# Layer 1's Hyena filter made in layer 1's mixing stage and kept on chip, both filters' inner layers made together

## The chip, the cores and the metric

The kernel runs on one core of a Trainium2 chip. The metric is the time of one execution on the device, in microseconds. The core's engines work side by side from queues in order: TensorE (PE, matrix products; its weight loads are PEld), VectorE (DVE), ScalarE (ACT), GpSimd (POOL) and SyncE (SP, which issues DMA loads). ACT also issues DMA stores.

## The reference

A trunk of two layers runs on two requests of 512 tokens, 1024 channels, with the same weights. Of each layer:

```python
h = _rmsnorm(x, norm_mix); proj = h @ w_in
q, k, v, g, hy_in, pool_in = jnp.split(proj, ...)
ret = _head_layernorm(_retention(q, k, v, logit_f, logit_b), ret_gn) * silu(g)
hy_out = _hyena(hy_in, ...)
pool_out = _pool_mixer(pool_in, pool_w, pool_scale)
x = x + concat([ret, hy_out, pool_out]) @ w_out
x = x + (gelu(dwconv3(h2 @ up_gate)) * (h2 @ up)) @ w_down      # h2 = _rmsnorm(x, norm_ffn)
x = x + sigmoid(x @ ple_gate_w) * _rmsnorm(p @ ple_w, ple_norm)
```

The Hyena group convolves 256 channels twice, by FFT, with filters that do not depend on the tokens. They come from a small network of each layer, and `khat` is their spectrum:

```python
h = sin(fr * (feats @ w1 + b1)); h = sin(fr * (h @ w2 + b2)); h = (h @ w3).reshape(L, 2, 2, 256)
h = h * exp(-t * deltas)
k_full = concat([h_f, 0, h_b[:0:-1]]); khat = rfft(k_full / sum(|k_full|))
```

Retention multiplies the scores of a head by decays `exp(dist * lg)`, which depend on the layer and head alone.

## The kernel before, in words

Every fp32 operand of a product is split into a high and a low f16 half, and a product is three matmuls (high by high, high by low, low by high; `mm3`, `pass3`). Weights of 128 x 1024 come by SP into `wraw` (4 buffers); ACT writes the high half and DVE the low one into `wspl` (9 buffers; `split`, lines 168 and 171). Tiles of 512 columns fp32 and halves of activations live in 72 buffers of the pool `gen`.

Each request has a `main_thread`, and side work has threads of its own: `filter_thread` and `decay_thread` of each layer, a `head_thread` per retention head, `hyena_thread`, `pool_thread`. All are generators. A planner (`schedule`) with a clock of its own takes the next step of the thread that is ready by planned times, and so writes the order of PE and of SP by hand; the order of DVE, ACT and POOL is set by the framework from the same program. A layer's tiles come in the order of `tile_order`: values `v00` to `v11` (PE: `vp`), then for heads 0 to 3 `q`, `k`, `g`, with the Hyena tiles `hy0` to `hy5` and the pooling tiles `pl0`, `pl1` between, the output tiles `o0` to `o7`, the gated FFN of both requests at once (`ffn_joint`), and the gate tiles `s0` to `s7` of the per-layer embedding.

A head: scores `sc`, times decays `st`, split `pt`, times values `ov`; then a layer norm over its 128 channels: ACT squares (`sq`), PE sums the columns (`cs`, line 753), DVE makes `rr`, PE spreads it (`rb`, line 763). The layer's own norm goes the same way, with `acc`, the sum of eight squares. Values are centred: `mu` and `vc` on DVE, high half of `v` on ACT, low half on DVE. The Hyena group transposes (`tp`), multiplies by Fourier matrices (`sp`), by `khat` on DVE, and back (`iv`).

`filter_thread(l)` loads feats, `fw` (w1, w2, b1, freq, b2) and w3, splits w3 (`w3s`), makes the first inner product (fp32, `fp`), then `sine` (six DVE operations and the sine on ACT), the second one and its sine, and splits the result (`h2`). Eight products with `w3s` follow; each is multiplied by `fdec` (`hfb`), its magnitudes are added (`fabs`, `ftot`), and sums and differences kept (`fs`, `fd`). A product with ones and a reciprocal give `frec`; the folds are multiplied by it and split (`folds`), and nine products with `fmat` give `khat`, written by ACT. Layer 0 makes its filter during its own mixing. Layer 1's is spawned by request 0's main thread of layer 0 at the tile named by `EARLY` (pl1); its nine `khat` of 256 KB are stored to DRAM (`ksp`) by ACT's queue, and `load_dft` loads them again by SP ahead of layer 1's first Hyena tile.

`decay_thread(l)` makes the tables of a layer, eight half heads: two DVE operations and an exponential on ACT for `dect`, and a store to DRAM (`ddec`) on ACT's queue. Layer 1's starts at planner time 425 (`run`: 25 + 400 l) and lies at about 465 to 517 us of the trace.

Of the kernel before, what the change touches and what calls it, by code (L numbers as in the profile page):

```python
# [16 lines left out]
F32 = mybir.dt.float32  # L17
# [14 lines left out]
JOINT = 3  # L32
HYW = 256
# [15 lines left out]
EARLY = "pl1"  # L49
# [47 lines left out]
def tile_order():  # L97

    names = ["v00", "v01", "v10", "v11"]
    for h, more in enumerate((["hy0", "hy1", "hy2", "hy3"], ["hy4", "hy5", "pl0"], ["pl1"], [])):  # L100
        names += [f"q{h}", f"k{h}", f"g{h}"] + more
    names += [f"o{m}" for m in range(NB)]
    for j in range(PLAIN):
        names += [f"fg{j}", f"fu{j}"]
    tiles, steps = list(names), list(names)
    pairs = []
# [15 lines left out]
    return tiles + more, steps + more  # L122
# [15 lines left out]
TILES, STEPS = tile_order()  # L138
TILE_AT = {n: i for i, n in enumerate(TILES)}
STEP_AT = {n: i for i, n in enumerate(STEPS)}  # L140
NT, NS = len(TILES), len(STEPS)


class Trunk:
# [54 lines left out]
    def plan_weights(self):  # L199
# [3 lines left out]
        for i in range(self.depth * NS):  # L203
            l, name = divmod(i, NS)
            name = STEPS[name]
# [24 lines left out]
    def prep(self, i):  # L230
# [5 lines left out]
        while k + 1 < len(self.at):  # L236

            frm = min(self.pos) if "." in STEPS[(k + 1) % NS] else i
# [16 lines left out]
    def wtile(self, l, last):  # L255
        self.live.append(l * NS + STEP_AT[last])
# [8 lines left out]
    def raw_names(self, j):  # L265

        return ("fg" + j[1:], "fu" + j[1:]) if j[0] == "f" else ("ea" + j[1:], "eb" + j[1:])
# [40 lines left out]
    def weight(self, l, name, *ss):  # L308
        i = l * NS + STEP_AT[name]
# [60 lines left out]
    def consts(self):  # L370
# [18 lines left out]
        self.ksp = self.dr.tile([9, 128, T], F32, name="ksp")  # L389
# [42 lines left out]
    def sine(self, a):  # L432

        k = self.g(name="sk")[0:64, :]
# [13 lines left out]
    def filter_thread(self, l, ev):  # L448
        nc, io = self.nc, self.io
        ft = self.g(name="feats")  # L450
        self.load(ft[0:33, :], io["feats"])
        fw = self.g(name="fw")
        self.load(fw[0:64, 0:132], io["fw"][l])
        w3 = []
        for o in range(2):
            w = self.g(name="w3")
            self.load(w[0:64, :], io["w3"][l][:, o * T:(o + 1) * T])
            q = self.g([128, 2, T], F16, name="w3s")
            self.split(q[0:64, 0], q[0:64, 1], w[0:64, :], WS)
# [4 lines left out]
        w1, w2, b1, fr, b2 = fw[0:33, 0:64], fw[0:64, 64:128], fw[0:64, 128:129], fw[0:64, 129:130], fw[0:64, 130:131]  # L464
        yield 0.0, 0.0
        a = self.g(name="fa")
        p = self.bank(name="fp")
        nc.tensor.matmul(p[0:64, :], w1, ft[0:33, :], start=True, stop=True)
        self.ts(a[0:64, :], p[0:64, :], b1, fr, ALU.add, ALU.mult)
        self.sine(a[0:64, :])  # L470
        yield 0.9, LAT["sin"][l > 0]
        a2 = self.g(name="fa2")
        p = self.bank(name="fp")
        nc.tensor.matmul(p[0:64, :], w2, a[0:64, :], start=True, stop=True)
        self.ts(a2[0:64, :], p[0:64, :], b2, fr, ALU.add, ALU.mult)
        self.sine(a2[0:64, :])
        a = None
        h2 = self.g([128, 2, T], F16, name="h2")
        self.split(h2[0:64, 0], h2[0:64, 1], a2[0:64, :])
        yield 0.9, LAT["sin"][l > 0]  # L480
# [62 lines left out]
        for i, (kind, pr, src) in enumerate(use):  # L543
# [19 lines left out]
        if l == 0:  # L563
            self.take_filters(kh)
# [89 lines left out]
    def load_dft(self, l):  # L654
        if l > 0:
            kh = {}
            for i, key in enumerate(FILTERS):
                kh[key] = self.g(name="khat")
                self.load(kh[key], self.ksp[i])
            self.take_filters(kh)  # L660
# [200 lines left out]
    def main_thread(self, s):  # L861
# [12 lines left out]
        for l in range(self.depth):  # L874
            vec = self.vec[l]
            h = []
            yield from self.h_steps(s, x, acc, vec[:, V_NMIX:V_NMIX + NB], h)
            x = None
            if s == 0 and l > 0:
                yield [self.ffn[l - 1].over]  # L880
            hw = self.hcw[l]
            mix = [None] * NB
            done = []
            hy, hev = [], [Event() for _ in range(6)]
            v = []
            for name in TILES[:TILE_AT["o0"]]:
                if name[0] == "v":
                    if name[2] == "0":
                        v.append([])
                        ps = self.values_early(l, h, s) if name == "v00" else [None, None]  # L890
                        for tp in range(2):
                            self.values(l, int(name[1]), h, s, tp, v[-1], ps.pop(0))
                            if ps or name != "v00":
                                yield (10.4 if name == "v00" else 5.2), 0.0
                    continue
                if name == "q0" and s == 0 and l > 0:
# [3 lines left out]
                p = self._proj(l, name, h, s)  # L900
                if name[:2] == "hy":
                    if name == "hy0" and s == 0:
                        self.load_dft(l)
                    j = int(name[2])
                    hy.append(self.conv3(p, hw, j, 6))
                    yield 5.15, 0.0
                    hev[j].set(self.clock + 3.0)
                    if j == 0:
                        done.append(Event())
                        self.spawn(self.hyena_thread(l, hy, hev, mix, done[-1]))  # L910
                elif name[:2] == "pl":
                    b = int(name[2])
                    if b == 0:
                        pw = self.g(name="poolw")
                        self.load(pw[:, 0:256], io["poolw"][l])
                    rc = self.g(name="rc")
                    self.load(rc, io["rcnt"][b])
                    m = self.pooling(p, b, rc)
                    yield 5.15, 0.0
                    done.append(Event())  # L920
                    self.spawn(self.pool_thread(l, b, m, None, pw[:, b * 128:(b + 1) * 128], mix, done[-1]))
                elif name[0] == "q":
                    qk = {"q": self.rotate(p)}
                    yield 5.15, 0.0
                elif name[0] == "k":
                    qk["k"] = self.rotate(p)
                    yield 5.15, 0.0
                else:
                    hd = int(name[1])
                    sg = self.g(name="sg")  # L930
                    self.act(sg, p, ACTF.Sigmoid, scale=1.0 / WS)
                    self.stt(sg, p, 1.0 / WS, sg, ALU.mult, ALU.mult)
                    if hd == 0:
                        yield [self.decay_ev[l]]
                    dec = self.dp.tile([128, 896], F32, tag="dec", name="dec")
# [542 lines left out]
```

## Time and profile before

| | us |
|---|---|
| runs | 2451.26, 2456.72, 2456.94 (median 2456.72) |
| profiled execution: its time | 2451.95 |
| its span | 2450.2 |
| PE busy | 2379.1 (97%) |
| DVE / ACT / POOL busy | 1779.5 / 1032.3 / 700.8 |
| mean DMA rate | 69 GB/s, 168.60 MB |

The span is what the profiler saw, from first to last instruction; the profiled execution took 1.75 us more. Engines overlap, so their busy times do not add up to the span. Mixing of layer 0 takes about the first 500 us, layer 1 begins at about 1246 us (its norm's column sum), its mixing ends near 1650. The granted clock of PE is given as a share of full speed.

### The profile page before, as it was taken

What the parts mean: (1) busy time and instruction counts of PE and PEld (TensorE: products, weight loads), DVE (VectorE), ACT (ScalarE), POOL (GpSimd) and SP (SyncE); (2) the same over time, 40 slices, a digit from 0 to 9 for tenths busy, and PEclk for the clock granted to TensorE, in tenths of its full rate; (3) what the DMA queues carried; (4) which work ended last, traced back from release to release, by engine and by line L of the source; (5) the groups of instructions that cost most, each with busy time, mean ns of one, the idle gap of its engine ahead of it and who ended that gap; (6) DMA issues with size and microseconds to landing.
All of it is one profiled execution on the core that took longest, in us unless ns stands there. A gap on an engine that the chain in (4) does not pass through costs nothing.

```text
span 2450.2 us, 30877 instructions
## 1 busy us (share of the span) xinstructions
PE 2379.1 (97%) x12024; PEld 1169.9 (48%) x12024; DVE 1779.5 (73%) x2526; ACT 1032.3 (42%) x1551; POOL 700.8 (29%) x528
## 2 busy tenths in 40 slices
PE   5999989999999999999999999999999999999997
PEld 4544654444444444444456555544444444444443
DVE  7994886968877868866575686554987786886655
ACT  4543334445534435444433343333553543544441
POOL 1213244124233333320121222510423334332011
PEclk8999999999999999999999999999999999999998
DMA  6122020341121121113232111032012112121301
GB/s 226 65 98 63 24 75 21 115 139 38 45 65 59 46 71 53 62 48 112 78 120 108 50 49 53 28 115 65 27 48 65 58 46 69 54 63 48 112 1 69
DMA packets 64363, 168.60 MB, mean 69 GB/s; under 512 B 7574, under 2 KB 13718, under 8 KB 64216
## 3 DMA queue, kind: packets, MB, share of 16 engines
q1 hardware_dynamic: 58312, 156.40, 19.3%
q10 hardware_dynamic: 5904, 10.23, 1.1%
q8 instruction: 94, 1.54, 0.3%
q14 instruction: 53, 0.43, 0.1%
HBM read 152.18 MB, written 14.42 MB: 68 GB/s over the span
## 4 chain that ended last, share of the span: by engine, by line
PE 74%; DVE 13%; issue 3%; ACT 2%; POOL 2%; DMA 0%; POOLq 0%; DVEq 0%; SPq 0%; ACTq 0%
PE fx L1183 13%; PE ex L1183 7%; PE fy L1183 7%; PE ey L1183 4%; PE fz L1183 3%; PE s L322 2%; PE o L323 2%; PE o L324 2%; PE o L322 2%; PE s L323 2%; PE s L324 2%; PE ez L1183 2%; DVE t L174 2%; DVE wspl L171 2%; DVE conv L171 2%
## 5 line engine op out<-in xcount | busy, mean ns | idle before, releaser
L1183 PEld LDWEIGHTS <-wspl 128*128 128x128 f16 x4704 | 461.1, 98 | 566.2 <-issue 13.7
L174 POOL TENSOR_TENSOR wraw<-wraw 128x512 f32<-128x512 f32 (+1 forms) x240 | 344.4, 1435 | 654.8 <-DVE wspl L171 640.7
L168 ACT ACTIVATE wspl<-wraw 128x1024 f16<-128x1024 f32 (+2 forms) x360 | 327.1, 910 | 370.8 <-POOL wraw L174 71.1
L171 DVE SCALAR_TENSOR_TENSOR wspl<-wraw,wspl 128x1024 f16<-128x1024 f32 (+2 forms) x360 | 395.5, 1100 | 82.6 <-ACT wspl L168 81.3
L1183 PE MATMUL fx<-hs,wspl 128*128 128x512 f16 x1368 | 312.3, 382 | 7.7 <-ACT r L168 7.7
L322 PEld LDWEIGHTS <-wspl 128*128 128x128 f16 x1536 | 152.1, 99 | 181.2 <-issue 6.9
L324 PEld LDWEIGHTS <-wspl 128*128 128x128 f16 x1536 | 150.6, 98 | 183.3 <-issue 3.3
L323 PEld LDWEIGHTS <-wspl 128*128 128x128 f16 x1536 | 150.7, 98 | 177.3 <-issue 3.6
L1183 PE MATMUL ex<-at,wspl 128*128 128x512 f16 x846 | 192.7, 379 | 0.0
L174 POOL TENSOR_TENSOR y<-t,mhalf 128x4 f32<-128x4 f32 x30 | 36.3, 1210 | 402.6 <-DVE t L178 402.5
L168 ACT ACTIVATE at<-conv 128x512 f16<-128x512 f32 x142 | 89.4, 629 | 143.7 <-DVE conv L174 111.8
L174 DVE TENSOR_TENSOR at<-conv,at 128x512 f16<-128x512 f32 x142 | 127.1, 896 | 26.2 <-ACT at L168 24.8
L171 DVE SCALAR_TENSOR_TENSOR conv<-r,scaled,conv 128x511 f32<-128x511 f32 x152 | 129.5, 852 | 2.1 <-ACT conv L168 0.4
L1183 PE MATMUL fx<-h,wspl 128*128 128x512 f16 x456 | 104.6, 379 | 0.0
L1183 PE MATMUL fy<-hs,wspl 128*128 128x512 f16 x456 | 104.6, 379 | 0.0
L1183 PE MATMUL fz<-h,wspl 128*128 128x512 f16 x456 | 104.6, 379 | 0.0
L1183 PE MATMUL fy<-h,wspl 128*128 128x512 f16 x456 | 104.6, 379 | 0.0
L168 ACT ACTIVATE sq<-x 128x512 f32<-128x512 f32 x80 | 49.2, 625 | 123.4 <-DVE x L171 66.3
L1183 PE MATMUL ey<-at,wspl 128*128 128x512 f16 x432 | 101.1, 379 | 0.0
L168 ACT ACTIVATE conv<-conv 128x512 f32<-128x512 f32 x88 | 55.3, 629 | 108.2 <-DVE conv L171 107.1
L174 DVE TENSOR_TENSOR acc<-acc,sq 128x512 f32<-128x512 f32 x84 | 62.6, 747 | 48.5 <-ACT sq L168 47.3
L324 PE MATMUL s<-xs,wspl 128*128 128x512 f16 x256 | 97.0, 379 | 0.0
(246 smaller groups left out, 4662.8 us busy)
## 6 DMA issues: line engine op xcount, KB each, us to landing
wraw<-in_w SPq DMA_DIRECT2D x172, 512.0 KB, 3.8
wraw<-in_w SPq DMA_DIRECT2D x48, 384.0 KB, 3.0
x<-in_x SPq DMA_DIRECT2D x32, 256.0 KB, 4.3
dec<-ddec SPq DMA_DIRECT2D x16, 448.0 KB, 4.6
wraw<-in_w SPq DMA_DIRECT2D x16, 256.0 KB, 2.6
xsp<-x ACTq DMA_DIRECT2D x16, 256.0 KB, 2.0
x<-xsp SPq DMA_DIRECT2D x16, 256.0 KB, 5.0
out_y<-out SPq DMA_DIRECT2D x16, 256.0 KB, 2.8
```

The lines of the kernel that those rows point to most:

```text
L168: return self.nc.scalar.activation(out=out, in_=in_, func=func, **k)
L171: return self.nc.vector.scalar_tensor_tensor(out=out, in0=in0, scalar=scalar, in1=in1, op0=op0, op1=op1)
L174: return (eng or self.nc.vector).tensor_tensor(out=out, in0=in0, in1=in1, op=op)
L322: self.nc.tensor.matmul(out, wv[:, 0, kb, :], x[:, 0], start=first, stop=False)
L323: self.nc.tensor.matmul(out, wv[:, 0, kb, :], x[:, 1], start=False, stop=False)
L324: self.nc.tensor.matmul(out, wv[:, 1, kb, :], x[:, 0], start=False, stop=last)
L1183: mm = lambda a, b, start=False, stop=False: self.nc.tensor.matmul(out, a, b, start=start, stop=stop, skip_group_check=not first)
```

## The change

The inner layers (w1, sine, w2, sine, split) of both filters are made at once in layer 0's filter thread: w1 of both layers side by side on 128 rows, w2 as blocks on the diagonal, one `fw` load of 128 x 259. `h2` of both layers is kept. Layer 1's filter thread starts with w3 and the first product with `w3s`; it is spawned in layer 1's own mixing, in request 0 at tile v10, and its `khat` stay on chip. In layer 1 the Hyena tiles come later: hy0 to hy3 after head 1, hy4, hy5, pl0 and pl1 after head 2. Layer 1's decay thread starts at planner time 1150. The code also gains a joint mixing of both requests (`mix_joint`, `TWINS`), which is off, since `TWINNED` is empty; `take` holds the steps of one tile that stood in `main_thread`.

```diff
-EARLY = "pl1"
+TWINNED = ()
+EARLY = "v10"
+LATER = 1125.0
...
-def tile_order():
+def tile_order(layer, twinned):
...
-    for h, more in enumerate((["hy0", "hy1", "hy2", "hy3"], ["hy4", "hy5", "pl0"], ["pl1"], [])):
+    late = ([], ["hy0", "hy1", "hy2", "hy3"], ["hy4", "hy5", "pl0", "pl1"], [])
+    for h, more in enumerate(late if layer else (["hy0", "hy1", "hy2", "hy3"], ["hy4", "hy5", "pl0"], ["pl1"], [])):
...
     def filter_thread(self, l, ev):
-        ft = self.g(name="feats")
-        self.load(ft[0:33, :], io["feats"])
-        fw = self.g(name="fw")
-        self.load(fw[0:64, 0:132], io["fw"][l])
+        rows = slice(l * 64, (l + 1) * 64)
+        if l == 0:
+            ft = self.g(name="feats")
+            self.load(ft[0:33, :], io["feats"])
+            fw = self.g(name="fw")
+            self.load(fw[:, 0:259], io["fw"])
         w3 = []
         for o in range(2):
             w = self.g(name="w3")
-            self.load(w[0:64, :], io["w3"][l][:, o * T:(o + 1) * T])
+            self.load(w[rows, :], io["w3"][l][:, o * T:(o + 1) * T])
             q = self.g([128, 2, T], F16, name="w3s")
-            self.split(q[0:64, 0], q[0:64, 1], w[0:64, :], WS)
+            self.split(q[rows, 0], q[rows, 1], w[rows, :], WS)
...
+        if l == 0:
+            w1, w2, b1, fr, b2 = fw[0:33, 0:128], fw[:, 128:256], fw[:, 256:257], fw[:, 257:258], fw[:, 258:259]
+            a = self.g(name="fa")
+            p = self.bank(name="fp")
+            nc.tensor.matmul(p, w1, ft[0:33, :], start=True, stop=True)
...
+            self.h2 = self.g([128, 2, T], F16, name="h2")
+            self.split(self.h2[:, 0], self.h2[:, 1], a2)
+            yield 0.9, LAT["sin"][0]
+        h2 = self.h2
...
-                self.pass3(p, h2[0:64, 0, jj], h2[0:64, 1, jj], w3[o][0:64, 0], w3[o][0:64, 1], True, True)
+                self.pass3(p, h2[rows, 0, jj], h2[rows, 1, jj], w3[o][rows, 0], w3[o][rows, 1], True, True)
...
-            if l > 0:
-                self.store(out=self.ksp[i], in_=kt)
-            else:
-                kh[kind, pr] = kt
+            kh[kind, pr] = kt
...
     def load_dft(self, l):
-        if l > 0:
-            kh = {}
-            for i, key in enumerate(FILTERS):
-                kh[key] = self.g(name="khat")
-                self.load(kh[key], self.ksp[i])
-            self.take_filters(kh)
...
+            for name in MIXING[l]:
+                if name == EARLY and s == 0 and l > 0:
+                    self.spawn(self.filter_thread(l, self.khat_ev[l]))
...
-                if name == EARLY and s == 0 and l + 1 < self.depth:
-                    self.spawn(self.filter_thread(l + 1, self.khat_ev[l + 1]))
...
-            self.spawn(self.decay_thread(l, self.decay_ev[l])).ready = 25.0 + 400.0 * l
+            self.spawn(self.decay_thread(l, self.decay_ev[l])).ready = 25.0 + LATER * l
```

How the order of the engines moves at two places follows. The first is ACT at the end of layer 0, where the squares of request 1's last two tiles feed the sum of the first norm of layer 1 (`sg` is the sigmoid of a gate tile, `s6` and `s7`; `xsp` a store). Before:

```order
L168 ACTIVATE sq_10522<-x_4856 128x512
L168 ACTIVATE sg_10552<-s6_10527 128x512
L168 ACTIVATE sq_10556<-x_4950 128x512
L184 DMA xsp_201<-x_4950 128x512
L168 ACTIVATE sg_10586<-s7_10561 128x512
L168 ACTIVATE sq_10590<-x_4995 128x512
L184 DMA xsp_201<-x_4995 128x512
L168 ACTIVATE v_10708<-vc_10706 128x512
```

In the changed program, from the square before (`sq_10185`) on:

```order
L181 ACT_TABLE_LOAD
L181 ACTIVATE dect_10173<-dect_10173 128x448
L181 ACT_TABLE_LOAD
L181 ACTIVATE sg_10215<-s6_10190 128x512
L197 DMA ddec_199<-dect_10173 128x448
L181 ACT_TABLE_LOAD
L181 ACTIVATE dect_10178<-dect_10178 128x448
L197 DMA ddec_199<-dect_10178 128x448
L181 ACTIVATE sq_10219<-x_4590 128x512
L197 DMA xsp_200<-x_4590 128x512
L181 ACT_TABLE_LOAD
L181 ACTIVATE sg_10249<-s7_10224 128x512
```

The exponentials of layer 1's decay tables, `dect`, stand between the squares and sigmoids, with four loads of ACT's tables of functions ahead of the last sigmoid.

The second place is DVE at the last values of layer 1 (`vp_10741` is one half of v10 of request 0), before:

```order
L738 TENSOR_REDUCE mu_10790<-vp_10741 128x4
L178 TENSOR_SCALAR mu_10790<-mu_10790 128x4
L171 SCALAR_TENSOR_TENSOR vc_10793<-vp_10741,mu_10790 128x512
L174 TENSOR_TENSOR v_10795<-vc_10793,v_10795 128x512
L738 TENSOR_REDUCE mu_10847<-vp_10798 128x4
L178 TENSOR_SCALAR mu_10847<-mu_10847 128x4
L171 SCALAR_TENSOR_TENSOR vc_10850<-vp_10798,mu_10847 128x512
L171 SCALAR_TENSOR_TENSOR hn_10864<-x_4426,vec1_94,rb_10855 128x512
L174 TENSOR_TENSOR v_10852<-vc_10850,v_10852 128x512
```

and in the changed program, where `vp_10414` is that tile:

```order
L745 TENSOR_REDUCE mu_10463<-vp_10414 128x4
L187 TENSOR_TENSOR v_10401<-vc_10399,v_10401 128x512
L191 TENSOR_SCALAR mu_10463<-mu_10463 128x4
L184 SCALAR_TENSOR_TENSOR vc_10466<-vp_10414,mu_10463 128x512
L187 TENSOR_TENSOR v_10468<-vc_10466,v_10468 128x512
L184 SCALAR_TENSOR_TENSOR w3s_10473<-w3_10471,w3s_10473 64x512
L184 SCALAR_TENSOR_TENSOR w3s_10478<-w3_10476,w3s_10478 64x512
L187 TENSOR_TENSOR hfb_10500<-fp_10496,fdec_10492 128x512
```

The low halves of w3 and the first `hfb` now stand behind the centred values, and the values of the next tile after them. PE in the changed program has at this place, with the end of `vp_10414` first:

```order
L341 LDWEIGHTS h_10170
L341 MATMUL vp_10414<-wspl_10273,h_10170 128x256
L342 LDWEIGHTS h_10170
L342 MATMUL vp_10414<-wspl_10273,h_10170 128x256
L340 LDWEIGHTS h2_529
L340 MATMUL fp_10496<-w3s_10473,h2_529 128x512
L341 LDWEIGHTS h2_529
L341 MATMUL fp_10496<-w3s_10473,h2_529 128x512
```

The first product of the filter follows directly on the tile `vp_10414`; before, the next `vp` did.

## Rows read from the trace of the kernel before

**Rows 1.** The page, first part: busy us (share of the span) of each engine.
```profile
PE 2379.1 (97%) x12024; PEld 1169.9 (48%) x12024; DVE 1779.5 (73%) x2526; ACT 1032.3 (42%) x1551; POOL 700.8 (29%) x528
```

**Rows 2.** PE's waits, whole run: releaser, us in total, times, longest.
```profile
PE cs L753 <- ACT sq L168: 11.4, 5, 3.8
```

**Rows 3.** Windows: busy us of each engine, granted clock, DMA share, GB/s.
```profile
350.00:375.00 25.00, 22.52 (x104) 10.20 (x103) 18.10 (x27) 9.34 (x15) 11.43 (x11) 0.93 0.26 90
400.00:425.00 25.00, 22.25 (x102) 9.54 (x101) 22.06 (x35) 9.62 (x16) 12.24 (x11) 0.97 0.08 22
425.00:450.00 25.00, 25.00 (x123) 11.51 (x122) 21.16 (x39) 9.73 (x17) 8.90 (x8) 0.97 0.37 134
1300.00:1400.00 100.00, 100.00 (x630) 60.50 (x628) 57.84 (x93) 36.58 (x54) 25.26 (x19) 1.00 0.27 96
```

**Rows 4.** PE's timeline: start us, us, line, operation [idle before <- releaser].
```profile
334.37 1.07 PE L468 MATMUL fp<-feats,fw 33*64 33x512 f32 x2
335.37 0.39 PE L327 MATMUL sc<-qk 128*128 128x512 f16 x1
...
359.26 1.05 PE L753 MATMUL cs<-ones,sq 128*128 128x1 f32 x8 [2.48 <-ACT sq L168]
...
422.36 1.05 PE L753 MATMUL cs<-ones,sq 128*128 128x1 f32 x8 [2.75 <-ACT sq L168]
...
466.25 0.56 PE L763 MATMUL rb<-identr,rr 128*128 128x128 f16 x7 [1.33 <-DVE rr L171]
...
1246.30 0.95 PE L753 MATMUL cs<-ones,acc 128*128 128x1 f32 x8
...
1279.41 1.02 PE L753 MATMUL cs<-ones,acc 128*128 128x1 f32 x8 [0.50 <-DVE acc L174]
...
1605.06 1.05 PE L753 MATMUL cs<-ones,sq 128*128 128x1 f32 x8 [1.70 <-ACT sq L168]
```

**Rows 5.** Tile `dect`: duration ns min/median/max, first and last start us.
```profile
L168 ACT ACTIVATE dect<-dect x16: 559/577/578, 85.3 to 516.4; 128x448 f32<-128x448 f32 x16
```

**Rows 6.** ACT's groups of instructions, whole run: busy us, mean ns, idle before.
```profile
L168 ACT ACT_TABLE_LOAD x15 | 19.2, 1283 | 3.0 <-PE g L324 1.5 <-PEq L1467 0.7 <-ACT khat L168 0.4
```

**Rows 7.** ACT's timeline at a table load and at the end of layer 0.
```profile
349.83 1.28 ACT L168 ACT_TABLE_LOAD   x1
351.13 0.63 ACT L168 ACTIVATE fa<-fa 64x512 f32<-64x512 f32 x1
...
1271.96 0.57 ACT L168 ACTIVATE sg<-s 128x512 f32<-128x512 f32 x1
...
1275.19 0.63 ACT L168 ACTIVATE sq<-x 128x512 f32<-128x512 f32 x1 [2.66 <-DVE x L174]
...
1277.91 0.63 ACT L168 ACTIVATE sq<-x 128x512 f32<-128x512 f32 x1 [1.60 <-DVE x L174]
```

**Rows 8.** DVE's timeline at layer 0's end and layer 1's values.
```profile
1273.76 0.68 DVE L174 TENSOR_TENSOR sg<-sg,e 128x512 f32<-128x512 f32 x1
...
1290.97 0.69 DVE L738 TENSOR_REDUCE mu<-vp 128x4 f32<-128x512 f32 x1 [2.23 <-PE vp L329]
...
1293.35 0.69 DVE L174 TENSOR_TENSOR v<-vc,v 128x512 f16<-128x512 f32 x1
```

**Rows 9.** DVE's groups of 300 to 600 us: low half of w3.
```profile
L171 DVE SCALAR_TENSOR_TENSOR w3s<-w,w3s 64x512 f16<-64x512 f32 x2 | 2.0, 980 | 2.2 <-ACT w3s L168 2.2
```

**Rows 10.** PE's waits of 100 to 300 us, layer 0's mixing.
```profile
PE sp L327 <- ACT u L168: 3.2, 2, 2.8
PE tp L598 <- DVE abs L174: 2.8, 2, 2.4
PE tp L598 <- ACT abs L168: 1.2, 1, 1.2
PE fp L510 <- DVE ftot L174: 1.1, 1, 1.1
```

**Rows 11.** PE's waits of 1285 to 1500 us, the same tiles of layer 1.
```profile
PE cs L753 <- ACT sq L168: 0.7, 1, 0.7
```

More of the change, by code (lines that the diff above doesn't have):

```diff
@@ L105, in tile_order @@
     tiles, steps = list(names), list(names)
+    if twinned:
+        both = [n for t in TWINS for n in t]
+        mixing = [n for n in mixing if n not in both]
+        steps = [n for n in steps if n not in both]
+        steps[4:4] = lace([f"m{i}" for i in range(len(TWINS))])
     pairs = []
@@ L121, in tile_order @@
     more = ["p0", "p1"] + [f"s{m}" for m in range(NB)]
-    return tiles + more, steps + more
+    return tiles + more, steps + more, mixing
 def step_time(name):
@@ L895, in main_thread @@
                     continue
+                if l in TWINNED and not M.done.owner and s == 1:
+                    M.done.owner = self
+                    yield [self.decay_ev[l]]
+                    yield from self.mix_joint(l, M)
+                    M.done.set(self.clock)
+                    yield 0.0, 0.0
+                elif l in TWINNED and M.done.time is None:
+                    yield [M.done]
                 if name == "q0" and s == 0 and l > 0:
                     self.load_rope()
-                if name == EARLY and s == 0 and l + 1 < self.depth:
-                    self.spawn(self.filter_thread(l + 1, self.khat_ev[l + 1]))
@@ L900, in main_thread @@
[L900 to L935, printed above, removed]
-                    nc.sync.dma_start(out=dec, in_=self.ddec[l, hd])
-                    yield 5.15, 0.0
-                    done.append(Event())
-                    self.spawn(self.head_thread(l, hd, qk, v, sg, dec, mix, done[-1]))
@@ L940, in main_thread @@
-            h = None
+                box = [self._proj(l, name, h, s)]
+                yield from self.take(l, s, name, box, M, 5.15)
+            h = M.h[s] = None
             if s == 1:
                 self.rope = None
+            mix, done = M.mix[s], M.ends[s]
             yield done
@@ L1039, in main_thread, with take @@
             nc.sync.dma_start(out=io["y"][s, m], in_=t)
+    def take(self, l, s, name, box, M, cost):
+        nc, io = self.nc, self.io
+        p = box.pop()
+        if name[:2] == "hy":
+            if not M.loaded:
+                M.loaded = True
+                self.load_dft(l)
+            j = int(name[2])
+            M.hy[s][j] = self.conv3(p, self.hcw[l], j, 6)
+            p = None
+            yield cost, 0.0
+            M.hev[s][j].set(self.clock + 3.0)
+            if j == 0:
+                M.ends[s].append(Event())
+                self.spawn(self.hyena_thread(l, M.hy[s], M.hev[s], M.mix[s], M.ends[s][-1]))
+        elif name[:2] == "pl":
+            b = int(name[2])
+            if b == 0:
+                M.pw[s] = self.g(name="poolw")
+                self.load(M.pw[s][:, 0:256], io["poolw"][l])
+            rc = self.g(name="rc")
+            self.load(rc, io["rcnt"][b])
+            m = self.pooling(p, b, rc)
+            rc = p = None
+            yield cost, 0.0
+            M.ends[s].append(Event())
+            self.spawn(self.pool_thread(l, b, m, None, M.pw[s][:, b * 128:(b + 1) * 128], M.mix[s], M.ends[s][-1]))
+        elif name[0] in "qk":
+            M.qk[s].setdefault(int(name[1]), {})[name[0]] = self.rotate(p)
+            p = None
+            yield cost, 0.0
+        else:
+            hd = int(name[1])
+            sg = self.g(name="sg")
+            self.act(sg, p, ACTF.Sigmoid, scale=1.0 / WS)
+            self.stt(sg, p, 1.0 / WS, sg, ALU.mult, ALU.mult)
+            p = None
+            if hd == 0 and self.decay_ev[l].time is None:
+                yield [self.decay_ev[l]]
+            dec = self.dp.tile([128, 896], F32, tag="dec", name="dec")
+            nc.sync.dma_start(out=dec, in_=self.ddec[l, hd])
+            yield cost, 0.0
+            M.ends[s].append(Event())
+            self.spawn(self.head_thread(l, hd, M.qk[s].pop(hd), M.v[s], sg, dec, M.mix[s], M.ends[s][-1]))
@@ new lines, in mix_joint @@
+    def mix_joint(self, l, M):
+        right = self.rights(M)
+        state = {}
+        self.load_rope()
+        for _, name in STEPS[STEP_AT[l, "m0.0"]:STEP_AT[l, f"m{len(TWINS) - 1}.6"] + 1]:
+            key, q = name.split(".")
+            q = int(q)
+            w = self.weight(l, name, 0, 1)
+            st = state.setdefault(key, {})
+            if q in (0, 1, 2):
+                st["XYZ"[q]] = self.bank(name="m" + "xyz"[q])
+            p = st["XYZXYXX"[q]]
+            self.product(p, w, right[q], q < 3)
+            i, s, box = 0, 0, []
+            if q in (0, 1, 3):
+                r = st[("r1", "r5", None, "r2")[q]] = self.g(name="r")
+                self.act(r, p)
+                r = None
+            elif q == 6:
+                i, box = 1, [p]
+                del state[key]
+            else:
+                n = {2: "r1", 4: "r2", 5: "r5"}[q]
+                self.tt(st[n], p, st[n], ALU.add)
+                i, s, box = int(q == 5), int(q > 2), [st.pop(n)]
+                if q < 5:
+                    del st["Z" if q == 2 else "Y"]
+            st = p = None
+            if box:
+                yield from self.take(l, s, TWINS[int(key[1:])][i], box, M, 2.58)
+            else:
+                yield 2.58, 0.0
@@ L1243, in run @@
         self.ffn = [Ffn() for _ in range(self.depth)]
+        self.mix = [Mix() for _ in range(self.depth)]
         a = self.spawn(self.main_thread(0))
```

106 lines of the change are left out of this document (55 added, 51 removed).

## The prediction

> **What bounds the kernel now.** The page's first part says that TensorE (PE) is busy for 2379.1 of 2450.2 us, and VectorE (DVE) for 73% [rows 1]. With 97% busy, the change can gain only what PE no longer computes, what it no longer waits, and the time after a wait in which its granted clock is low. So I read the waits of PE next. The largest between the start and the end is the column sum `cs` of a layer norm behind ScalarE's (ACT) square `sq`: five times, 11.4 us, longest 3.8 [rows 2]. Then the windows of 25 us around the stretch in which layer 1's filter is now made: the granted clock is 0.93 in one and 0.97 in two, and 1.00 in layer 1's mixing [rows 3]. Each such drop follows a PE wait; a mean of 0.93 over 25 us loses 0.07 x 25 = 1.75 us of full clock (2.4 GHz; the lower level is 1.2). A wait of 2.5 us therefore costs over 4 us. Last, PE's timeline row by row, for the waits that the change can remove or make [rows 4].
>
> One bound once: 0.3% of the median is 7.4 us, about what a measurement of this kernel can tell from no change. The sum is made against the profiled execution, 2451.95 us. It is 4.8 us under the median of the runs, 2456.72; the runs lie at 2451 and at 2457, and I cannot tell at which of these a new median lands, so I add half of 4.8, 2.4 us, at the end.
>
> **What goes away in layer 0.** (a) The two inner fp32 products of layer 1's filter. From the first one's start, 334.37, to the next operation's, 335.37, is 1.00 us on PE [rows 4]; the joint ones have twice the rows and the same columns, so they cost what layer 0's cost. Two: -2.0. (b) The wait of 2.48 before `cs` at 359.26. Its `sq` stands on ACT behind work that came late from DVE, which holds the sine's seven operations in that stretch; with the sine gone I take the whole wait and its clock drop [rows 3, 4]: 2.48 + 1.75 = -4.2. (c) The wait of 2.75 before `cs` at 422.36. Layer 1 has the same place without a filter, at 1605.06, and waits 1.70 there [rows 4]. So 1.05 goes, and the drop: 0.97 in two windows, 0.03 x 50 = 1.5 [rows 3]. -2.6. (d) The wait of 1.33 for `rb` at 466.25, whose input `rr` stands on DVE behind the filter's folds: -1.3. The wait at the first FFN tiles comes after the filter's end; I take nothing for it. Sum of layer 0: **-10.1**.
>
> The nine stores and nine reloads of `khat` (2.3 MB each way) count for nothing: no wait in the rows read is for `khat`, and in layer 1's mixing the loads of w3, bias, fdec and fmat (2.3 MB) take the reloads' place on SP's queue, while PE is 100.00 of 100 us busy there [rows 3]. If SP were late, it would show as weights late (`wspl`), which no wait of PE names. The two columns of fw more and the kept h2 buffer cost nothing that PE sees.
>
> **What comes in at the layer boundary.** decay_thread(1) now starts at planner time 1150 and lands under the end of layer 0. Per half head it brings two DVE operations, one exponential of 577 ns on ACT and a store on ACT's queue [rows 5]. The changed order of ACT shows four ACT_TABLE_LOAD rows around these exponentials and the sigmoids of request 1's last two gate tiles; before there were none here. A load takes 1283 ns [rows 6], and in the timeline the next activation starts 1.30 after the load's start [rows 7].
> - First norm of layer 1, request 0: `cs` at 1246.30 does not wait before [rows 4]. One load or a pair of DVE operations stands ahead of its last sum: +1.3 (0 to 3).
> - Second norm, request 1, `cs` at 1279.41, waiting 0.50 before [rows 4]. Four loads and two exponentials are 4 x 1.28 + 2 x 0.58 = 6.3 us more on ACT. ACT idled 2.66 and 1.60 there [rows 7], but this idle time lies behind the sigmoids, and the loads stand ahead of them, each on the chain sigmoid, product, sum, square, `acc`. The first sigmoid, with two loads and an exponential (3.1) ahead of it, ended at 1272.53 before, and DVE took it up at 1273.76 [rows 7, 8]: 1.2 of slack, so it comes 1.9 late. The second has the same ahead of it, and the slack again: another 1.9. Together 3.8. A wait of 4.3 then draws a drop of the clock, 1.75: +5.5 (0, if all fits into the idle 4.3, to 6.3 + 1.75).
> - The filter's first product `fp`. PE has it directly behind the 48 products of a `vp`, and DVE has the low half of w3 behind `mu`, `vc` and `v` of that same `vp`. Before, this chain runs from 1290.97, where `mu` waited for PE, to the end of `v` at 1294.04: 3.07 us [rows 8]; the low half of w3 takes 980 ns more [rows 9]. PE stands still for 3.07 + 0.98 = 4.0, and a drop follows: +5.7 (4.0 without the drop, 6.6 if the second half's 0.98 gets ahead too). This wait is the part of the sum I am surest of, since both queues are in order; `vp`'s and `g`'s products queued behind `fp` on PE wait with it.
>
> **What comes in inside layer 1's mixing.** The filter's work on DVE (eight `hfb` and their sums, the reciprocal, the folds) goes where DVE was busy for 58 of 100 us [rows 3], beside PE, and the khat reloads' buffers come free for it. Its eight `fp`, the sum and nine `fmat` products move with it and cost the same there. Two places stay open. `rr` behind folds again, as in (d): between 0 and 1.3, I take +0.7. And the last head's tail: the wait of 1.70 at 1605.06 goes, because other products now stand before `cs`, but `ov` comes directly behind its `sc`, whose decays and splits (`st`, `pt`) I guess at the size of that same wait or somewhat more: +0.7 (-1.7, nothing in its place, to +1.7, twice as long).
>
> Losses: 1.3 + 5.5 + 5.7 + 0.7 + 0.7 = **+13.9**. Net +3.8: 2451.95 + 3.8 = 2455.8, plus 2.4 gives **2458**. Its own range is 2451 to 2464, by the ends above.
>
> **The rivals.**
> - *Only the gains* (faster). The loads fall into ACT's idle time and w3 is split before it is needed, so the boundary's 12.5 vanish: 2458 - 12.5 = **2446**. For it: ACT idles 4.3 us there [rows 7]. Against it: both queues at `fp` are in order. Chance 0.20.
> - *Layer 1 takes on layer 0's waits* (slower). Layer 0 makes its filter in its own mixing, and PE waits there from 100 to 300 us for 3.2 + 2.8 + 1.2 + 1.1 = 8.3 us at `sp`, `tp` and `fp`; in layer 1, with the filter elsewhere, PE waits 0.7 from 1285 to 1500 [rows 10, 11]. If the filter is the reason, layer 1 gets 8.3 - 0.7 + one drop 1.75 = 9.3 in place of my 0.7: 2458 + 8.6 = **2467**. It decides if `tp` and `sp` of layer 1 wait over 6 us together. Against it: DVE has 42 us idle of 100 in layer 1 [rows 3], and its Hyena tiles come later than layer 0's. Chance 0.13.
> - *The gains of (b) to (d) fail*, because request order and not the filter sets those waits: the 8.1 stay, **2466**. For it: the `cs` wait at 1605.06 arises without any filter. Against it: it is shorter, 1.70 [rows 4]. Chance 0.11.
> - *A table switch costs twice its load.* If each of the four held ACT 1.28 longer, +5.1: **2463**. Against it: the next activation stands straight behind the load [rows 7]. Chance 0.06.
>
> The Trainium skill, "ScalarE: Activation LUTs", section "What ACT_TABLE_LOAD costs", adds a drain of about 1.38 us to a load of 1.28, some 2.66 us a switch, which would give that last rival's time; its load agrees with 1283 ns here, the drain does not show in these rows.
>
> **How the numbers follow.** The forecast has 0.50. "Same" is 2449.3 to 2464.1: the forecast and the table rival, 0.56. Faster is the rival with only gains, 0.20. Slower are the second and third, 0.24. The range 2446 to 2468 leaves out about half of the gains-only case (0.10) and the upper parts of the two slower ones (about 0.08).
>
> **What would show it.** Right: no wait at 359 and under 2 us at 420 and none at 465; a `cs` wait of 3 to 5 us behind ACT or DVE at the second norm of layer 1, and an `fp` wait of about 4 us behind w3s a little later, with the clock below 1.00 in both windows. Wrong: no wait at `fp`; granted clock 1.00 through the boundary; or waits of `sp` and `tp` over 3 us each in layer 1.

## The result, and the profile after

| | before | changed |
|---|---|---|
| median, us (6 runs each) | 2454.16 (2450.15 to 2457.15) | 2468.97 (2467.05 to 2471.32) |
| ratio | | 1.0060, 95% interval 1.0049 to 1.0070 |
| profiled execution / its span, us | 2451.95 / 2450.2 | 2469.39 / 2467.6 |

The change makes the kernel slower by 0.6%, some 15 us. Three executions of before lie near 2451 and three near 2457, the profiled one among the lower, so the two profiled executions differ by 17.4. The page's first part, beside [rows 1], shows PE as the bound as before; its busy time grew by 7.8 us, although it has two products (four instructions) fewer:

```profile
PE 2386.9 (97%) x12020; PEld 1174.4 (48%) x12020; DVE 1768.8 (72%) x2511; ACT 1040.7 (42%) x1557; POOL 707.1 (29%) x528
```

Three marks on PE's timeline cut the two spans into stretches: the first product of each layer's FFN and the first norm of layer 1. For before, 1246.30 stands in [rows 4]; the other two marks, with the idle time ahead of them:

```profile
617.02 1.51 PE L1183 MATMUL fx<-hs,wspl 128*128 128x512 f16 x5 [3.86 <-ACT r L168]
...
1781.77 2.72 PE L1183 MATMUL fx<-hs,wspl 128*128 128x512 f16 x6 [2.65 <-ACT r L168]
```

The changed kernel, PE's timeline at these marks (588.88, 1219.76 and 1799.98) and at the waits that [rows 4] has of before:

```profile
412.11 1.05 PE L760 MATMUL cs<-ones,sq 128*128 128x1 f32 x8 [1.66 <-ACT sq L181]
...
588.88 1.69 PE L1245 MATMUL fx<-hs,wspl 128*128 128x512 f16 x5 [2.67 <-ACT r L181]
...
1219.76 1.05 PE L760 MATMUL cs<-ones,acc 128*128 128x1 f32 x8 [1.69 <-DVE acc L187]
...
1259.40 1.84 PE L760 MATMUL cs<-ones,acc 128*128 128x1 f32 x8 [5.23 <-DVE acc L187]
...
1365.22 0.56 PE L770 MATMUL rb<-identr,rr 128*128 128x128 f16 x7 [2.55 <-DVE rr L184]
...
1465.15 1.05 PE L760 MATMUL cs<-ones,sq 128*128 128x1 f32 x8 [1.38 <-ACT sq L181]
...
1799.98 2.35 PE L1245 MATMUL fx<-hs,wspl 128*128 128x512 f16 x8 [2.67 <-ACT r L181]
```

| stretch | before, us | changed, us | difference |
|---|---|---|---|
| start to layer 0's FFN | 617.0 | 588.9 | -28.1 |
| layer 0's FFN to layer 1's first norm | 629.3 | 630.9 | +1.6 |
| layer 1's mixing, to its FFN | 535.5 | 580.2 | +44.7 |
| layer 1's FFN to the end | 668.4 | 667.6 | -0.8 |

Some 18 to 20 us of PE work went from the first stretch to the third: 24 products with `w3s` and 54 with `fmat`, 0.216 us from start to start, are 16.8, and the product with ones and small work come to it. What is left over is a gain of 8 to 10 in layer 0 and a loss of 25 to 27 in layer 1. PE's waits in layer 1's mixing, where [rows 11] and [rows 4] have 0.7, 0.50 and 1.70 in all:

```profile
PE cs L760 <- DVE acc L187: 6.9, 2, 5.2
PE fp L340 <- ACT w3s L181: 3.5, 1, 3.5
PE rb L770 <- DVE rr L184: 2.5, 1, 2.5
PE ov L341 <- DVE pt L187: 1.4, 2, 1.0
PE cs L760 <- ACT sq L181: 1.4, 1, 1.4
PE fp L341 <- DVE w3s L184: 0.3, 1, 0.3
PE sp L340 <- ACT u L181: 1.2, 4, 0.4
PE tp L611 <- DVE abs L187: 0.7, 1, 0.7
PE tp L611 <- ACT abs L181: 0.4, 1, 0.4
```

Waits are only part of it. The windows of 25 us show the granted clock, the third number from the end. In layer 0 the windows of [rows 3] are at 1.00 now (400 to 450 too), but two others are lower in this execution; at the boundary of the layers 1250 to 1300 has 0.81 and 0.92:

```profile
150.00:175.00 25.00, 24.64 (x122) 12.32 (x123) 19.58 (x34) 10.29 (x17) 6.07 (x5) 0.88 0.00 1
275.00:300.00 25.00, 20.35 (x125) 11.97 (x124) 17.71 (x35) 9.67 (x17) 2.53 (x2) 0.93 0.00 1
350.00:375.00 25.00, 25.00 (x120) 11.76 (x118) 17.22 (x25) 10.94 (x18) 13.39 (x12) 1.00 0.09 30
1200.00:1225.00 25.00, 23.31 (x111) 10.83 (x110) 22.15 (x37) 13.15 (x18) 7.29 (x5) 0.93 0.34 114
1250.00:1275.00 25.00, 15.96 (x104) 12.05 (x102) 15.81 (x31) 12.04 (x16) 1.01 (x2) 0.81 0.53 192
1275.00:1300.00 25.00, 25.00 (x161) 15.90 (x159) 15.97 (x29) 9.20 (x15) 7.17 (x6) 0.92 0.00 1
1450.00:1475.00 25.00, 23.62 (x130) 13.04 (x129) 16.63 (x31) 6.99 (x11) 6.21 (x6) 0.93 0.07 22
```

Before, the first of these two windows of layer 0 is at 0.93, and the second at 1.00:

```profile
275.00:300.00 25.00, 20.13 (x136) 12.44 (x134) 19.08 (x37) 9.17 (x16) 3.35 (x3) 1.00 0.00 1
```

By the prediction's own conversion the boundary loses (0.07 + 0.19 + 0.08) x 25 = 8.5 us of full clock, and 1450 to 1475 another 1.75. In layer 0 the drops of (b) and (c), 3.25, are gone, and two others, 0.05 and 0.07 over 25 us, cost 3.0 in this execution. That the change makes these two is not shown. In eight of the nine other runs with the wider sine, 150 to 175 is at 0.93, as before, and in the ninth at 1.00. In all nine 275 to 300 is low (0.90 to 0.93), but it is at 0.93 too in a run of the kernel before (the one with the decay alone moved, below), behind a wait of 2.76 that was 2.75 before:

```profile
275.00:300.00 25.00, 20.12 (x120) 11.78 (x119) 17.99 (x36) 8.83 (x16) 3.34 (x3) 0.93 0.00 1
```

The chain behind the wait of 5.23 is on ACT, in the order that stands ahead of the prediction. Between one square and the last, four loads of 1.28 and two exponentials of 0.58 stand, and each activation starts within 0.03 us of a load's end:

```profile
1247.18 0.61 ACT L181 ACTIVATE sq<-x 128x512 f32<-128x512 f32 x1
1247.81 1.28 ACT L181 ACT_TABLE_LOAD   x1
1249.11 0.58 ACT L181 ACTIVATE dect<-dect 128x448 f32<-128x448 f32 x1
1249.70 1.28 ACT L181 ACT_TABLE_LOAD   x1
1250.99 0.60 ACT L181 ACTIVATE sg<-s 128x512 f32<-128x512 f32 x1
1251.61 1.28 ACT L181 ACT_TABLE_LOAD   x1
1252.90 0.58 ACT L181 ACTIVATE dect<-dect 128x448 f32<-128x448 f32 x1
...
1253.88 0.63 ACT L181 ACTIVATE sq<-x 128x512 f32<-128x512 f32 x1 [0.40 <-ACT dect L181]
...
1254.53 1.28 ACT L181 ACT_TABLE_LOAD   x1
1255.82 0.60 ACT L181 ACTIVATE sg<-s 128x512 f32<-128x512 f32 x1
1257.90 0.63 ACT L181 ACTIVATE sq<-x 128x512 f32<-128x512 f32 x1 [1.48 <-DVE x L187]
```

The chain behind the wait at `fp` starts on DVE, where `mu` waits for the end of `vp` and `vc` follows. From there both queues hold w3 up: ACT has its high half behind the high half of `v`, DVE its low half behind the low half of `v`. The first matmul of `fp` takes the high half and waits 3.50 for ACT; the second waits 0.30 more for DVE:

```profile
1270.73 0.63 ACT L181 ACTIVATE v<-vc 128x512 f16<-128x512 f32 x1 [4.87 <-DVE vc L184]
1271.39 1.14 ACT L181 ACTIVATE w3s<-w 64x512 f16<-64x512 f32 x2
...
1268.61 0.69 DVE L745 TENSOR_REDUCE mu<-vp 128x4 f32<-128x512 f32 x1 [3.40 <-PE vp L342]
...
1270.01 0.69 DVE L184 SCALAR_TENSOR_TENSOR vc<-vp,mu 128x512 f32<-128x512 f32 x1
1271.40 0.69 DVE L187 TENSOR_TENSOR v<-vc,v 128x512 f16<-128x512 f32 x1 [0.69 <-ACT v L181]
1272.12 1.29 DVE L184 SCALAR_TENSOR_TENSOR w3s<-w,w3s 64x512 f16<-64x512 f32 x2
```

### The profile page after: what moved, and what is told of

It reads as the page before. It is cut to its first block, busy times and chain, and to the rows that moved or that the text cites. A ratio compares the mean times of both kernels' runs of the same rounds, so it can differ in the third digit from the quotient of the medians.

```text
span 2467.6 us, 30823 instructions
## 1 busy us (share of the span) xinstructions
PE 2386.9 (97%) x12020; PEld 1174.4 (48%) x12020; DVE 1768.8 (72%) x2511; ACT 1040.7 (42%) x1557; POOL 707.1 (29%) x528
## 4 chain that ended last, share of the span: by engine, by line
PE 76%; DVE 16%; ACT 3%; issue 3%; DMA 1%; POOL 0%; SPq 0%; ACTq 0%; POOLq 0%; DVEq 0%
PE fx L1245 14%; PE ex L1245 7%; PE fy L1245 7%; PE ey L1245 4%; PE fz L1245 4%; PE o L335 2%; PE o L336 2%; PE o L337 2%; DVE t L187 2%; PE ez L1245 2%; DVE wspl L184 2%; PE s L337 2%; PE s L336 2%; PE s L335 2%; DVE conv L184 2%
## 5 line engine op out<-in xcount | busy, mean ns | idle before, releaser
L1245 PEld LDWEIGHTS <-wspl 128*128 128x128 f16 x4704 | 461.0, 98 | 564.4 <-issue 11.8
L187 POOL TENSOR_TENSOR wraw<-wraw 128x512 f32<-128x512 f32 (+1 forms) x240 | 351.0, 1463 | 645.8 <-DVE wspl L184 631.7
L184 DVE SCALAR_TENSOR_TENSOR conv<-r,scaled,conv 128x511 f32<-128x511 f32 x152 | 136.7, 899 | 2.9 <-ACT conv L181 1.2
L187 DVE TENSOR_TENSOR at<-conv,at 128x512 f16<-128x512 f32 x142 | 118.9, 838 | 27.3 <-ACT at L181 26.0
L337 PE MATMUL s<-xs,wspl 128*128 128x512 f16 x256 | 97.8, 382 | 0.0
L336 PE MATMUL s<-xs,wspl 128*128 128x512 f16 x256 | 97.7, 382 | 0.0
```

What stands on the lines that cost most here:

```text
L184: return self.nc.vector.scalar_tensor_tensor(out=out, in0=in0, scalar=scalar, in1=in1, op0=op0, op1=op1)
L187: return (eng or self.nc.vector).tensor_tensor(out=out, in0=in0, in1=in1, op=op)
L336: self.nc.tensor.matmul(out, wv[:, 0, kb, :], x[:, 1], start=False, stop=False)
L337: self.nc.tensor.matmul(out, wv[:, 1, kb, :], x[:, 0], start=False, stop=last)
L1245: mm = lambda a, b, start=False, stop=False: self.nc.tensor.matmul(out, a, b, start=start, stop=stop, skip_group_check=not first)
```

## The experiments

Each of them was compared with the kernel before on the same chip; before had medians of 2452 to 2454 in these comparisons. A difference between two experiments carries these 2 us as its uncertainty.

**Is it the decay tables at the boundary?** One constant of the changed kernel goes back:

```diff
-LATER = 1125.0
+LATER = 400.0
```

> The changed kernel with layer 1's decay thread at planner time 425 again, as before the change. Theory 1 (the waits at the layer boundary come from the decay tables): the first cs wait (1.69) goes, the second falls from 5.23 to about 0.5, and the half-clock stretches behind them go (3.4 us at half clock, 1.7 lost, and 6.8, 3.4 lost): 1.7 + 4.7 + 1.7 + 3.4 = 11.5 less than the changed kernel's 2469, about 1 us back in layer 0: 2458. Theory 2 (layer 1's own mixing is overloaded by the filter, waits only move along): within 3 us of the changed kernel, 2466 or more, with longer waits at fp, rb, tp or sp.

2456.85 us, ratio 1.0011 (1.0002 to 1.0019): 12 us less than the changed kernel, by one constant. The second `cs` waits 0.5, as before; what stays is the wait for w3, 3.0 and 0.4:

```profile
PE cs L760 <- DVE acc L187: 0.5, 1, 0.5
```

Theory 1 holds, and theory 2 falls for this part: the waits did not move along.

**Table loads, or the work itself?** The changed kernel with a copy in the exponential's place (it leaves the exponential out):

```diff
-                self.act(d, d, ACTF.Exp)
+                self.act(d, d, ACTF.Copy if l else ACTF.Exp)
```

> The changed kernel with a copy in place of the exponential in layer 1's decay tables (the exponential is left out there), so that ACT does the same number of operations of the same length, and DVE and the queues too, but loads no tables at the boundary. If the table loads make the wait at the second cs: it falls from 5.23 to under 2, the time to about 2460. If the decay's DVE operations and exponentials themselves do: the wait stays over 3.5, the time over 2465.

2461.34 us, ratio 1.0033 (1.0020 to 1.0046), 7.6 less than the changed kernel. None of the nine loads that the changed kernel has from 1215 to 1260 is left. The two waits of `cs` fall from 6.9 together to 2.8, the longer one to 1.9, and the wait for w3 stays at 3.5:

```profile
PE cs L760 <- DVE acc L187: 2.8, 2, 1.9
```

So about two thirds of the 12 us are the loads. The rest is what else the decay brings to this place (operations on DVE and ACT, stores), which these runs do not part. The Trainium skill, "ScalarE: Activation LUTs", section "Rules for kernel authors", says to group functions by table set and do all of one set before switching; here the scheduler of ACT mixed exponentials and sigmoids, and this run puts 7.6 us on that mixture.

**Does the price need the rest of the change?** The kernel before with the decay thread alone moved:

```diff
-            self.spawn(self.decay_thread(l, self.decay_ev[l])).ready = 25.0 + 400.0 * l
+            self.spawn(self.decay_thread(l, self.decay_ev[l])).ready = 25.0 + 1146.0 * l
```

> The kernel before with layer 1's decay thread alone moved, to planner time 1171, where the order of ACT has the same four table loads around the last two sigmoids of request 1 as in the changed kernel. Theory 1 (the price is that of the place, whatever the filter does): the two cs waits at the boundary come as in the changed kernel, and the time is 11 to 12 over before, 2465. Rival (they come only together with the filter's work there): under 2458.

2466.66 us, ratio 1.0053 (1.0038 to 1.0069), 13 to 15 us over before: the rival falls, and theory 1 holds for the place. The waits at the boundary are the same two:

```profile
PE cs L753 <- DVE acc L174: 6.4, 2, 5.5
```

That is 5.9 more wait than before at this place, and the clock there (0.86) loses 3.5. But not all of the 15 arises at the boundary. The profiled execution is 14.9 longer than that of before, and 5.3 of it are there at layer 0's FFN, 622.31 in place of 617.02, where this kernel's waits are nearly those of before:

```profile
622.31 1.01 PE L1183 MATMUL fx<-hs,wspl 128*128 128x512 f16 x2 [3.82 <-ACT r L168]
...
1252.71 1.05 PE L753 MATMUL cs<-ones,acc 128*128 128x1 f32 x8 [0.94 <-DVE acc L174]
```

At 294.96 both executions are still level; what comes between is the clock. The wait at 359, 2.49 as in [rows 4], drew 0.86 where before it drew 0.93:

```profile
350.00:375.00 25.00, 22.51 (x98) 10.74 (x97) 18.32 (x27) 9.39 (x15) 11.79 (x10) 0.86 0.27 90
1285.00:1310.00 25.00, 19.53 (x137) 14.73 (x136) 15.69 (x31) 9.32 (x13) 1.31 (x2) 0.86 0.35 122
```

A drop after the same wait thus cost 1.75 us in one execution and 3.5 in another. From layer 0's FFN to the end this kernel is 9.5 longer than before: 5.9 is the wait, the rest clock. Its fastest execution, 2460.50, is some 10 over the lower ones of before. So the place costs some 9.5 without the rest of the change, against 12 within it; that the 5.3 of layer 0 come from moving the decay is not shown.

**The first product of the filter.** Put off by 12 us of planner time:

```diff
-        yield 0.0, 0.0
+        yield 0.0, 12.0 * l
         if l == 0:
```

> The changed kernel with layer 1's first filter product 12 us of planner time after the split of w3 instead of at once. Theory 1: the wait for w3s (3.50 + 0.30) and the half-clock stretch behind it (6.8 us, 3.4 lost) go: 7.2 less than the changed kernel, 2462; the cs wait of 5.2 before it stays. Theory 2: PE waits as long at another place of the filter, the time within 3 us of the changed kernel.

2473.80 us, ratio 1.0084 (1.0070 to 1.0098), 5 more than the changed kernel. I expected 2462: the wait for w3 went, but the last `sp` of the layer waited 7.2 where none had waited over 0.4, and a `cs` behind `sq` 4.1 instead of 1.4:

```profile
PE sp L340 <- ACT u L181: 7.2, 1, 7.2
```

Theory 2 is nearer: PE waits as long at other places, and the time passed even its 3 us. Why is not shown. `khat` was written 4 to 6 us later than in the changed kernel (from 1406.5 to 1452.9, against 1400.8 to 1449.3), no wait names it, and the `sp` that waits comes at 1550, behind the last `u`; PE's order there is another one. The other way to take the wait away leaves PE's order as it is and brings only the split forward, on top of the early decay:

```diff
-EARLY = "v10"
+EARLY = "v00"
...
-        yield 0.0, 0.0
+        yield 0.0, 4.0 * l
         if l == 0:
```

> As the run with the decay early (2457), and layer 1's filter thread spawned at v00 with 4 us of planner time before its first product: TensorE's order is the same, only w3's load and split come ahead of the values on ACT and DVE. Theory 1 (the wait at fp is the split's place in the two queues and nothing else): 3.02 + 0.42 of wait and 6.8 us at half clock (3.4) go, 2450. Theory 2 (layer 1's DVE is overloaded, the wait moves along): 2455 or more.

2451.12 us, ratio 0.9989 (0.9979 to 1.0000), 5.7 less than with the decay early alone (on another chip); no wait of PE is left at the boundary, and the waits inside the mixing are what they were (`rb` 2.6, `cs` 1.4, `ov` 1.4). Theory 1 holds: it was the split's place in two queues.

**The tile order.** Layer 1 in the order of before, the rest as in the changed kernel:

```diff
-    for h, more in enumerate(late if layer else (...)):
+    for h, more in enumerate(late if layer > 1 else (...)):
```

> The changed kernel with layer 1's tiles in the order of before (hy0 to hy3 after head 0). If the later Hyena tiles only give the filter time and cost nothing: the Hyena work comes before khat is there, the planner puts other work in between, and the time is within 3 us of the changed kernel or up to 5 us more. If the new order itself costs the small waits of layer 1 (rb 2.55, cs 1.38, sp and tp 2, ov 1.4): these go and the time falls by 5 or more, to 2464.

2480.85 us, ratio 1.0110 (1.0095 to 1.0126), 12 more. Neither number was expected: with the early Hyena tiles PE waits at the transposes,

```profile
PE tp L611 <- ACT abs L181: 8.6, 4, 3.3
```

where the changed order waits 0.4. One of the four waits, 1.37 at 1365, has the filter's folds ahead of it on DVE. The other three, 7.2 together, come at 1500 to 1510, after the last `khat` (1456.6): there the `iv` products of both requests run as one block (1478 to 1490), PE runs two more tiles, and the transposes then wait for the Hyena group's own steps on DVE and ACT, which do no work of the filter any more. In the changed order other tiles lie between the two requests' blocks. The later Hyena tiles are worth 12 us once the filter is in this layer.

**The inner layers alone**, with layer 1's filter, tile order and decay as before (its `khat` over DRAM; the diff is the change's own, with the other parts taken back):

> The kernel before with one part of the change alone: the inner layers of both filters made together in layer 0's thread; layer 1's filter stays in layer 0, its khat go over DRAM, the tile order and the decay's start are those of before. Theory 1 (terms a and b of the prediction): two products, 2.0, and the wait of 2.48 at 359 with its half clock, 1.7, go: 6.2 less; the wider sine adds 0.8 of wait at the transposes at 147 and 3.4 us more at half clock (1.7), as the changed kernel shows: 2.5 back. About 2449. Rival (that wait is not the sine's): within 2 us of before.

2458.35 us, ratio 1.0022 (1.0011 to 1.0033): slower, against both theories. The wait at 359 is gone, but without its sines the filter of layer 1 runs some 45 us earlier in layer 0 (its reciprocal on DVE at 404.29 in place of 448.73). DVE then works through the reciprocal and the folds, the `st` of a head stand behind them, and one `cs` behind ACT waits 15.65 us:

```profile
436.14 1.86 PE L771 MATMUL cs<-ones,sq 128*128 128x1 f32 x8 [15.65 <-ACT sq L181]
```

This run does not price the inner layers; it moved the filter. So they were taken apart where the filter stays in layer 1: as in the run with w3 split ahead, with layer 0's inner layers alone on 64 rows as before, and a thread of its own at pl1 of layer 0 for both on 128 rows:

```diff
+                if name == "pl1" and s == 0 and l + 1 < self.depth:
+                    self.spawn(self.inner_thread())
```

> As the run with w3 split ahead (2451), but layer 0's filter makes its own inner layers on 64 rows as before, and both layers' are made again on 128 rows at pl1 of layer 0, where before had them. Theory 1 (terms a and b): two more products, 2.0, and the wait of 2.48 at 359 with its half clock, 1.7, come back: 2457; less 2.5 if the wider sine is what lengthens the waits at 147: 2455. Rival (they cost nothing there once layer 1's filter is elsewhere): 2451 within 2.

2454.68 us, ratio 1.0008 (0.9999 to 1.0016), 3.6 more than with them together and near theory 1's 2455. The wait behind the sine came back, if shorter, and without a drop of the clock (350 to 375 stays at 1.00):

```profile
359.55 1.05 PE L786 MATMUL cs<-ones,sq 128*128 128x1 f32 x8 [1.95 <-ACT sq L181]
```

and the wait at the transposes at 147 us is 2.4 there, where the kernels with the wider sine have 3.2. Two products, 2.0, and 1.95 of wait, less 0.8, are 3.2 of the 3.6; the clock term of (b) is not confirmed by this run.

**Can both kernels be beaten?** Three steps on the run with w3 split ahead. First, folds on GpSimd:

```diff
-                self.tt(t, t, rec, ALU.mult)
+                self.tt(t, t, rec, ALU.mult, nc.gpsimd if l and i else None)
```

> As the run before, and in layer 1 four of the nine multiplications of folds by the reciprocal go from DVE to GpSimd, which is 24 to 27% busy there. If the rb wait of 2.5 is DVE's folds in front of rr: it goes, 2.5 less than the run before. If rr is late for another reason, or GpSimd shares what DVE needs: the wait stays over 1.5 and the time is the same within 1.

2454.58 us, ratio 1.0005 (0.9995 to 1.0014), 3.5 more. The wait grew to 4.9, with 0.9 more behind it, since GpSimd also makes `y`, the power between `t` and `rr`, and that operation on 128 x 4 numbers stood behind three folds and then took 6.61 us beside a busy DVE:

```profile
1336.08 4.80 POOL L187 TENSOR_TENSOR fold<-fold,frec 128x512 f32<-128x512 f32 x3
1340.85 6.61 POOL L187 TENSOR_TENSOR y<-t,mhalf 128x4 f32<-128x4 f32 x1
```

Second, the decay at another place (`LATER = 1040.0` in place of 400):

> As the run with w3 split ahead (2451), with the decay thread at planner time 1065, before the gate tiles of layer 0, where no norm waits for ACT. If only the place at the norm is dear: no cs wait at the boundary, layer 0's mixing has 13 us less on DVE, 2449 to 2451. If table loads and stores late in layer 0 cost anywhere: 2455 or more.

2450.96 us, ratio 0.9990 (0.9981 to 0.9998). It loads tables between sigmoids there as well, and no `cs` waits at the boundary: with no norm behind ACT the loads cost nothing that can be seen. Third, the folds later:

```diff
-        yield 0.9, LAT["recip"][l > 0]
+        yield 0.9, LAT["recip"][l > 0] + 5.0 * l
```

> As the run with the decay at planner time 1065 (2451), and layer 1's filter waits 5 us of planner time more between the reciprocal and the folds, so that rr of head 1 stands ahead of all folds on DVE. If the rb wait of 2.6 and its drop of the clock come from the folds: both go, 2447. If khat then comes too late for the first Hyena products (the rival, as 12 us later at the start cost 7.2 at sp): sp waits 2 or more and the time stays at 2451 or above.

2448.38 us, ratio 0.9984 (0.9974 to 0.9994): the `rb` wait is gone, `sp` is not late (0.8), and part of the gain is given back at `ov`:

```profile
PE ov L341 <- DVE pt L187: 4.6, 4, 2.8
```

This version is faster than before by 0.16% and than the changed kernel by about 19 us (0.9984 against 1.0060).

## Why the prediction was wrong

It forecast no change that can be told, 2458, and the kernel became slower, 2469, just outside the range of 2446 to 2468. (The sum's own range, 2451 to 2464, does not follow from its ends: taken together they give 2447 to 2465.) The sum forecast 3.8 more than the profiled execution of before, and the changed one has 17.4 more. By its steps, against the profile:

| step | predicted | profile and runs |
|---|---|---|
| (a) two products | -2.0 | -2.0 (two fewer; not seen by itself) |
| (b), (c), (d) waits | -2.48, -1.05, -1.33 | gone, 1.66 left of (c), gone |
| (b), (c) clock | -3.25 | gone; +3.0 by two other drops, not shown to be the change's |
| wider sine | 0 | +0.8 of wait at 147 |
| first norm | +1.3 | 1.69, and 1.75 of clock |
| second norm | +5.5 | 4.7 more, and about 3.4 of clock |
| `fp` behind w3 | +5.7 | 3.8, and about 3.4 of clock; by experiment 5.7 |
| layer 1's mixing | +1.4 | about 7 |

**The mechanisms** were in the main the ones named. The waits of layer 0 went as the steps (b) to (d) say, 1.66 for 1.70 in (c), and the gain there, 8 to 10 by the stretches, is near the 10.1 forecast. The `cs` wait at the second norm came behind the four loads, 5.2 for 4.3. The wait at `fp` came at the place stated, 3.8 for 4.0, but the prediction looked at DVE alone: 3.50 of it is for the high half of w3 on ACT, which it left out, and 0.30 for DVE's low half. That the sizes agree so well is in part luck, since both halves stand behind the same `vc`.

**The steps that failed** are two terms that were mis-sized. First, the price of a clock drop at the boundary: I took 1.75 for the second norm and for `fp` each and none for the first norm, 3.5 together, and the granted clock lost 8.5 there. With 1.2 more of wait the boundary cost 18.7 in place of 12.5. (The step "the joint ones ... cost what layer 0's cost" looked only at PE, too; on DVE the wider sine stands in front of the transposes of layer 0 by 0.8 us more, and the run with the inner layers apart shows both sides, 2.4 against 3.2 of wait.) Second, the mixing of layer 1, +1.4. I named two places and bounded them by 1.3 and 1.7; the profile has `rb` 2.55, `cs` 1.38 with a drop of 1.75, `sp` and `tp` 2.3, `ov` 1.4, against 2.4 before: 7 us. For `rb` I took half of layer 0's 1.33; the last run shows that it was the folds' place ahead of `rr`. The two terms are 11.8 of the 13.6 that the sum is short; the rest, 1.8, may be layer 0's gain of 8 to 10 in place of 10.1.

**The rivals.** Only the gains: fell; 2446 was not reached even with the decay and w3's split moved (2451, and 2448 with the folds later). Layer 1 takes on layer 0's waits: fell by its own point, `tp` and `sp` wait 2.3 together, not over 6; but its direction was right, and the run with the old tile order has 8.6 at `tp`: the change's tile order is what averted it. The gains fail: fell. A table switch costs twice: fell, since the next activation starts 1.30 us after the load's start and the wait was made by four loads of 1.28. The slower outcome came by none of these, but by larger prices on the steps of the forecast.

**The part that decides** is one constant. Moved back in the changed kernel, the decay gives 12 of its 15 us, and moved alone in the kernel before it costs some 9.5 at the boundary (13 to 15 by the medians); w3's split gives 5.7 more. Without the two the rest of the change is worth 0.1% at most.

## What to carry to other kernels

Work that "fits anywhere" because its engine is 40% busy must not be put in front of a reduction that the bound engine waits for: the nine table loads among the squares and sigmoids ahead of two norms cost 7.6 us here, and loads 85 us of planner time earlier, with no norm behind ACT, cost nothing that can be seen. When a producer is moved next to its consumer, give the consumer's inputs a place ahead in the in-order queues, without moving the consumer: the split ahead gave 5.7 us, the consumer 12 us later lost 4.8. And price a wait of TensorE by range: behind the same wait the clock drop cost nothing or 1.75 us in one place and 1.75 or 3.5 in another.

## What was not expected of the hardware

The same wait did not draw the same drop: 2.48 us before `cs` at 359 left 0.93 in its window before, and 2.49 left 0.86 in the run with the decay moved; 2.75 before `sp` at 294.96 left 1.00 before, and 2.76 left 0.93 in that run. Waits of 1.69 and 1.38 us, at 1219.76 and 1465.15 of the changed kernel, drew drops (0.93), while in [rows 4] the wait of 1.70 at 1605.06 drew none, and 1.71 at that place drew one (0.93) in the run with the decay moved. What separates them was not tried. In the run with the decay moved, layer 0 came out 5.3 us longer with nearly the same waits.

GpSimd's power on 128 x 4 numbers took 6.61 us beside DVE's fold work, against 1210 ns on the average of thirty before. The Trainium skill, "SBUF — State Buffer", section "Who interferes with whom", says that a DVE instruction with two inputs in SBUF contends with a GpSimd instruction that reads SBUF, and that the order of issue decides which of the two blocks. These rows agree with it, but no run here took DVE's work away to show it.
